# Decoder layer: 18 of 32 gate pairs with seven products, their weight sums made ahead into DRAM scratch

## The chip, the cores and the metric

The kernel runs on one NeuronCore of a Trainium2 chip. The metric is the device time of one execution, in microseconds (us). TensorE is called PE below, VectorE DVE, ScalarE ACT, GpSimd POOL and SyncE SP, as in the profile.

## The reference

One layer of a decoder trunk over T = 16 + 256 positions of width 2048, all in float32:

```python
h = h + 0.5 * swiglu(rms_norm(h, g1), w_gate1, w_up1, w_down1)      # 2048 -> 5632 -> 2048
z = rms_norm(h, g2) @ w_in
q, k, v, qi, ki, wi, xc, gate_b, gate_c, ga, gc = split(z)
y_attn = dsa_sparse_attention(q, k, v, qi, ki, wi, 64) @ w_attn_branch   # indexer, top 64 keys, softmax
y_conv = (gate_b * causal_depthwise_conv(gate_c * xc, conv_w, conv_b)) @ w_conv_branch
h = h + (sigmoid(ga) * y_attn + sigmoid(gc) * y_conv) @ w_out
h = h + 0.5 * swiglu(rms_norm(h, g3), w_gate2, w_up2, w_down2)
return h[:, 16:]
```

The part that matters here is `ga` and `gc`: two projections, 2048 to 2048 each, of the 256 sequence positions, and their merge with the two branch outputs.

## The kernel before, in words

**Weights.** Every weight is streamed from DRAM once, as tiles of 128 partitions x 2048 float32 (1 MiB; 1536 for 768 KB), through three raw buffers, issued on SP's queue (L203). `Stream.split` turns a raw tile, a unit of 128 x 1024 at a time, into a high part `whi` (ACT, L251) and the remainder `wlo` (DVE, L252); a product of weights and activations is then three matmuls (`mac3`, L636 to L638: high by high, high by low, low by high). There are four buffers each for `whi` and `wlo`, and `Stream.next`, called when PE's program comes to a new unit, splits up to three units ahead. What else is to be done is put in lists with a due unit: `early` work is issued before the split of that call, `later` work behind it. All engines run their queues in order.

**Stages.** ffn1 (feature-major, 272 positions wide), the projections for keys, values, indexer and queries with the attention work spread between them, the gated convolution, the gates with the two branch projections, the output projection, ffn2.

**The gates stage.** Four groups c = 0 to 3, each 512 columns of both gates: `pairs_gate(c)` lists eight pairs of row blocks. A pair is a 2 x 2 block product, for two tiles of 128 tokens. A pair of kind `C` is done plainly: 8 block products, 24 matmuls of 512 columns, two units of weights, into the PSUM banks q2, q3, q4, q8. A pair of kind `S` is done with seven products (a Strassen-Winograd scheme): 21 matmuls over three and a half units, 6 matmuls to a full unit, into q1, q5, q6, q7 and q2, q3, q4. It needs sums of the weights, made from the loaded tile by DVE (`sum_ahead`, L223 to L230), and sums of the activations (`made`, made once for each pair index, `sums_of_tokens`). After the last such pair of a group, `recombine` folds the four sum banks into four SBUF tiles: ACT copies q1 (L713), then DVE, one step a unit, reads q6 (L715), q7 (L716), q5 (L717) and q5 again (L718). Behind a group follow 8 units of branch projections (`pbr`, 12 matmuls a unit) into q1, q5 and q6, q7; then `merge` (L1223), issued as early work of the next unit, multiplies these four banks in that order with the sigmoids, and L1225 adds. In groups 1 to 3, between the halves of the seventh pair (n == 6), PE transposes the former group's merged tile into two banks (L683), which ACT and DVE then read out.

**Kind P.** ffn2 has pairs of kind `P` besides: their four weight sums are made ahead, during ffn1, by `Stream.prepare`: a tile is fetched on POOL's queue (L179), DVE adds 4 times 128 x 512 (L183), POOL's queue stores the sums to DRAM scratch (L186). When the pair's turn comes, the 1 MiB of sums and 768 KB of the plain weights are loaded, and there is nothing left to add. Three tiles rotate in `prepare`; a fetch is issued two sets ahead, and the work is spread evenly over the units between two given ones.

The seven products of a pair are issued in this order, where `P` swaps two of them so that q1 is done before q2:

```python
todo7 = [("q7", t3), ("q5", t1), ("q6", t2), ("q3", b22), ("q1", b11), ("q4", t4), ("q2", b21)]
if kind == "P":
    todo7[4:6] = todo7[5:3:-1]
```

Of the kernel before, what the change touches and what calls it, by code (L numbers as in the profile page):

```python
# [24 lines left out]
H = 8  # L25
# [35 lines left out]
SEVEN = (3, 5, 7)  # L61
SEVEN2 = (3, 5, 7, 1)
DOUBLES = 2
SIDE = 6
# [6 lines left out]
def pairs_gate(c):  # L71
    return list(zip("CCCSCSCC", range(PAIRS)) if c == 0 else zip("CSSCSCCC", [0, 3, 5, 1, 7, 2, 4, 6]))
# [24 lines left out]
class Stream:  # L97
# [28 lines left out]
    def add_pair(self, kind, four, five, ahead=None):  # L126

        if kind == "C":
            self.add(four.pop(0), 4, WIDE)
            return  # L130
        if kind == "P":
            src, made = ahead.pop(0)
            self.ahead_of.append(src)
            self.made_ahead.append(made)
            self.add(made, 4, WIDE)
            self.add(src[:, WIDE:], 3, WIDE)
            return
        g = len(self.loads)
        at = 1
        if kind == "D":  # L140
            src, at = five.pop(0), 0
            self.loads.append((src[:, 2 * WIDE :], 3 * WIDE))
            self.added[g] = len(self.doubles)
            self.doubles.append((g, src))
# [62 lines left out]
    def sum_ahead(self):  # L207

        add = self.nc.vector.tensor_add
        for g, kind, _, _, _ in self.subs[self.n_split : self.n_split + 2]:  # L210
            if kind == "sa" and self.sum_pool and g not in self.summed:
# [4 lines left out]
                if g in self.added:  # L216
                    sa, one, last = self.sums[g, "sa"], raw[:, :WIDE], raw[:, 2 * WIDE : 3 * WIDE]
                else:
                    sa, one, last = (
                        self.lent if self.lent is not None else self.sum_pool.tile([P, 2 * WIDE], F32, name="sa", tag="sa"),  # L220
                        raw[:, WIDE : 2 * WIDE], raw[:, 3 * WIDE :],
                    )
                    add(  # L223
                        sa.rearrange("p (q c) -> p q c", q=2),
                        raw[:, WIDE : 3 * WIDE].rearrange("p (q c) -> p q c", q=2),
                        raw[:, :WIDE].rearrange("p (q c) -> p q c", q=1).to_broadcast([P, 2, WIDE]),
                    )
                    self.sums[g, "sa"] = sa
                add(sb[:, :WIDE], sa[:, WIDE:], one)
                add(sb[:, WIDE:], sb[:, :WIDE], last)  # L230
                self.sums[g, "sb"] = sb

    def split(self, upto):
        nc = self.nc
        while self.n_split < min(upto, len(self.subs)):
# [21 lines left out]
            if kind == "sa" and g in self.added:  # L257
# [51 lines left out]
def tile_decoder_layer(  # L309
# [15 lines left out]
    wg: bass.AP,  # L325
    wb: bass.AP,
# [418 lines left out]
    with ExitStack() as mix:  # L745
# [8 lines left out]
        ys = mp.tile([P, H, 2, SEQ], F32R, name="ys")  # L754
        cs = [mp.tile([P, KC // 2, 2, SEQ], F32R, name=f"cs{i}", tag=f"c{i}") for i in range(2)]
# [352 lines left out]

        CV0 = META - 2
# [61 lines left out]
        st.sum_pool = gp  # L1171
# [3 lines left out]
        for at, (i, to) in zip((0, 3, 16), made1.items()):  # L1175
# [16 lines left out]
        def gates(c):  # L1192
# [3 lines left out]
            def after_end(q, buf, tags):  # L1196
# [12 lines left out]
                lambda n: n == 6 and c > 0 and turn_merged(("q6", "q1")), None, after_end,  # L1209
# [22 lines left out]
        st.sum_pool = None  # L1232
# [182 lines left out]
    "h", "small", "rope", "cbias", "ident", "wgu1", "wd1", "wk", "wkw", "wv", "wqi", "wq", "wcv", "wg", "wb",  # L1415
# [30 lines left out]
def _quads(kind, w0, w1, i, j0, j1):  # L1446
# [4 lines left out]
        {"C": [a12, a11, a22, a21], "S": [a21, a11, a22, a12], "P": [a21, a22, a11, a12], "D": [a21, a21, a11, a22, a12]}[kind], 1  # L1451
# [3 lines left out]
def _by_kind(chunks):  # L1455
    return [np.stack([x for k, x in chunks if k in kinds]) for kinds in ("CS", "D", "P")]


def _gates(ga, gc):
    return np.stack([_quads(k, ga, gc, i, c, c) for c in range(D // WIDE) for k, i in pairs_gate(c)])  # L1460


def _second(wg, wu, wd):
# [8 lines left out]
    return _by_kind(res)  # L1472
# [25 lines left out]
def _layout(x, meta_tokens, ffn1_norm_g, ffn1_w_gate, ffn1_w_up, ffn1_w_down, mix_norm_g, w_in, q_norm_g,  # L1498
# [29 lines left out]
    a["wg"] = _gates(ga, gcv)  # L1528
# [26 lines left out]
```

## Time and profile before

| | us |
|---|---|
| median of 3 runs | 2134.0 (2133.54 to 2134.19) |
| the profiled execution | 2133.74 |
| its span | 2131.9 |
| PE busy | 2118.5 |
| DVE busy | 1580.6 |
| ACT busy | 1100.0 |

In the span, ffn1 lies at 0 to 793 us, the key, value, indexer and query projections at 793 to 925, the convolution at 925 to 1087, the gates with the branches at 1087 to 1344, the output projection to 1435, and ffn2 behind it. Rows of the timeline give the start in the span, the duration, the engine, the line and the operation with output and inputs; idle time before it and who ended it stand in brackets. Windows give for each stretch its length, then busy time and count of instructions by engine, granted clock, share of the DMA engines and GB/s. Matmuls are pipelined: the duration of one is longer than the distance from one start to the next.

### The profile page before, as it was taken

The page shows a single profiled execution, that of the slowest core. Times are in us where ns is not written, and L with a number is a line of the kernel's source. Part 1 is how long each engine was busy: PE and PEld are TensorE (multiplying, and loading weights), DVE is VectorE, ACT ScalarE, POOL GpSimd, SP SyncE. Part 2 cuts the span into 40 slices and gives each one's busy share as a digit, 9 for nine tenths or more (in the row PEclk, how much of TensorE's full clock was granted, in tenths as well). Part 3 has the DMA queues.
Part 4 walks back from the last instruction along what each step waited for, and adds up shares of the span by engine and source line. Part 5 has one row for each costly group of instructions (what it writes and reads, how often), then busy time and mean ns, then how long its engine had stood idle before and what let it go on. Part 6 is the DMA issues. An engine that isn't in the chain of part 4 may idle for free.

```text
span 2131.9 us, 32318 instructions
## 1 busy us (share of the span) xinstructions
PE 2118.5 (99%) x13015; PEld 1911.0 (90%) x13015; DVE 1580.6 (74%) x2047; ACT 1100.0 (52%) x1421; POOL 97.6 (5%) x146
## 2 busy tenths in 40 slices
PE   8999999999999999999999999999999999999999
PEld 8999999999999999889988888888888888888887
DVE  7766666666666756577678778587888878888887
ACT  6444433344444445465455555467665566655564
POOL 3000000000000100000000000010000000000000
PEclk9999999999999999999999999999999999999999
DMA  7778888787888854544455565567787887788774
GB/s 283 267 296 308 309 311 298 296 310 306 311 298 296 311 204 165 178 139 159 158 178 188 188 217 195 174 228 251 287 295 243 278 293 275 253 251 304 264 257 148
DMA packets 79927, 531.44 MB, mean 249 GB/s; under 512 B 8896, under 2 KB 9024, under 8 KB 24352
## 3 DMA queue, kind: packets, MB, share of 16 engines
q1 hardware_dynamic: 65088, 432.30, 56.1%
q0 software_dynamic: 14544, 96.89, 13.6%
q8 instruction: 102, 1.67, 0.3%
q14 instruction: 49, 0.40, 0.1%
q10 hardware_dynamic: 144, 0.17, 0.0%
HBM read 483.20 MB, written 46.14 MB: 248 GB/s over the span
## 4 chain that ended last, share of the span: by engine, by line
PE 97%; DVE 1%; ACT 1%; POOL 1%; DMA 0%; issue 0%; SPq 0%; DVEq 0%
PE q L637 13%; PE q L638 13%; PE q L636 13%; PE pd L429 4%; PE pd L430 4%; PE pd L428 4%; PE pg L428 4%; PE pu L428 4%; PE pu L429 4%; PE pg L429 4%; PE pg L430 4%; PE pu L430 4%; PE po L443 3%; PE po L445 1%; PE pbr L636 1%; PE pbr L638 1%
## 5 line engine op out<-in xcount | busy, mean ns | idle before, releaser
L252 DVE TENSOR_TENSOR wlo<-raw,whi 128x1024 fp32r<-128x1024 f32 (+1 forms) x837 | 969.6, 1171 | 504.2 <-ACT whi L251 492.9
L251 ACT ACTIVATE whi<-raw 128x1024 fp32r<-128x1024 f32 (+1 forms) x837 | 842.7, 1015 | 896.7 <-PE q L638 261.1
L636 PE MATMUL q<-whi,act 128*128 128x512 f32 x783 | 305.9, 391 | 0.0
L637 PE MATMUL q<-wlo,act 128*128 128x512 f32 x783 | 305.0, 390 | 0.0
L638 PE MATMUL q<-whi,act 128*128 128x512 f32 x783 | 304.7, 389 | 0.0
L428 PE MATMUL pd<-mid,whi 128*128 128x272 f32 x704 | 201.7, 286 | 0.0
L429 PE MATMUL pd<-mid,whi 128*128 128x272 f32 x704 | 201.7, 286 | 0.0
L430 PE MATMUL pd<-mid,wlo 128*128 128x272 f32 x704 | 201.7, 286 | 0.0
L428 PE MATMUL pg<-act,whi 128*128 128x272 f32 x672 | 192.7, 287 | 0.0
L429 PE MATMUL pg<-act,whi 128*128 128x272 f32 x672 | 192.5, 287 | 0.0
L430 PE MATMUL pg<-act,wlo 128*128 128x272 f32 x672 | 192.5, 286 | 0.0
L428 PE MATMUL pu<-act,whi 128*128 128x272 f32 x672 | 192.5, 286 | 0.0
L429 PE MATMUL pu<-act,whi 128*128 128x272 f32 x672 | 192.5, 286 | 0.0
L430 PE MATMUL pu<-act,wlo 128*128 128x272 f32 x672 | 192.5, 286 | 0.0
L637 PEld LDWEIGHTS q<-wlo,act 128*128 128x128 f32 x783 | 147.1, 188 | 30.8 <-DVE wlo L252 0.9
L638 PEld LDWEIGHTS q<-whi,act 128*128 128x128 f32 x783 | 147.0, 188 | 30.3
L636 PEld LDWEIGHTS q<-whi,act 128*128 128x128 f32 x783 | 147.1, 188 | 30.0
L428 PEld LDWEIGHTS pd<-mid,whi 128*128 128x128 f32 x704 | 132.6, 188 | 0.0
L429 PEld LDWEIGHTS pd<-mid,whi 128*128 128x128 f32 x704 | 132.6, 188 | 0.0
L430 PEld LDWEIGHTS pd<-mid,wlo 128*128 128x128 f32 x704 | 132.6, 188 | 0.0
L429 PEld LDWEIGHTS pg<-act,whi 128*128 128x128 f32 x672 | 126.6, 188 | 0.0
L428 PEld LDWEIGHTS pg<-act,whi 128*128 128x128 f32 x672 | 126.6, 188 | 0.0
(283 smaller groups left out, 3800.4 us busy)
## 6 DMA issues: line engine op xcount, KB each, us to landing
raw<-in_wgu_dram SPq DMA_DIRECT2D x87, 1024.0 KB, 6.1
raw<-in_w_dram SPq DMA_DIRECT2D x74, 1024.0 KB, 6.8
raw<-in_wd_dram SPq DMA_DIRECT2D x44, 1024.0 KB, 6.0
prep<-in_w2p_dram POOLq DMA_DIRECT2D x42, 1024.0 KB, 9.0
sums<-prep POOLq DMA_DIRECT2D x42, 1024.0 KB, 5.5
raw<-sums SPq DMA_DIRECT2D x42, 1024.0 KB, 5.2
raw<-in_wg_dram SPq DMA_DIRECT2D x32, 1024.0 KB, 4.8
raw<-in_w2p_dram SPq DMA_DIRECT2D x42, 768.0 KB, 5.0
```

Of the source, the lines that this page charges most:

```text
L251: nc.scalar.activation(to[0], raw, AF.Copy)
L252: nc.vector.tensor_sub(to[1], raw, to[0].bitcast(F32))
L428: nc.tensor.matmul(ps, whi, xhi, start=first, stop=False)
L429: nc.tensor.matmul(ps, whi, xlo, start=False, stop=False)
L430: nc.tensor.matmul(ps, wlo, xhi, start=False, stop=last)
L443: nc.tensor.matmul(ps.rearrange("p (a t) -> p a t", a=2), whi, x(i), start=i == 0, stop=False)
L445: nc.tensor.matmul(ps[:, :SEQ], wlo, x(i)[:, 0, :], start=False, stop=i == total - 1)
L636: nc.tensor.matmul(ps, xhi, whi, start=n == 0, stop=False)
L637: nc.tensor.matmul(ps, xhi, wlo, start=False, stop=False)
L638: nc.tensor.matmul(ps, xlo, whi, start=False, stop=n == total - 1)
```

## The change

Kind `S` is gone: all pairs with seven products in the gates are now of kind `P`, and there are more of them: three of eight in group 0 (before two), five of eight in each of groups 1 to 3 (before three). The order of the pairs changes with it; groups 1 to 3 now begin with two `P`, and the last one with seven products is the sixth of its group (before the fifth, in group 0 the sixth both times). Sums of activations are made for two more pair indices, 1 and 6, during group 0. `prepare` has 60 sets in place of 42: the 18 of the gates and the first 33 of ffn2's during ffn1, ffn2's last 9 during the key and query projections, in the memory that `cs` and `ys` take afterwards. The transposes of the merged tile go to q1 and then q6, in place of q6 and then q1.

```diff
-SEVEN = (3, 5, 7)
+SEVEN = (3, 5, 7, 1, 6)
+LATE = 9
...
 def pairs_gate(c):
-    return list(zip("CCCSCSCC", range(PAIRS)) if c == 0 else zip("CSSCSCCC", [0, 3, 5, 1, 7, 2, 4, 6]))
+    return list(zip("CCCPPPCC", [0, 2, 4, 3, 5, 7, 6, 1]) if c == 0 else zip("PPCPPPCC", [3, 5, 0, 7, 1, 6, 2, 4]))
...
-    def prepare(self, pool, u0, u1):
+    def prepare(self, tile_of, n0, n1, u0, u1):
...
-        todo = list(zip(self.ahead_of, self.made_ahead))
+        todo = list(zip(self.ahead_of, self.made_ahead))[n0:n1]
...
-                if g in self.added:
-                    sa, one, last = self.sums[g, "sa"], raw[:, :WIDE], raw[:, 2 * WIDE : 3 * WIDE]
-                else:
...
-                add(sb[:, :WIDE], sa[:, WIDE:], one)
-                add(sb[:, WIDE:], sb[:, :WIDE], last)
+                add(sb[:, :WIDE], self.sums[g, "sa"][:, WIDE:], raw[:, :WIDE])
+                add(sb[:, WIDE:], sb[:, :WIDE], raw[:, 2 * WIDE : 3 * WIDE])
...
         for kind, _ in pairs_gate(c):
-            st.add_pair(kind, wg_c, [])
+            st.add_pair(kind, wg_c, [], wg_p)
...
-            st.prepare(fp, 14, units1 - 12)
+            st.prepare(
+                lambda i: fp.tile([P, RAW], F32, name="prep", tag="prep", bufs=3),
+                0, len(st.ahead_of) - LATE, 14, units1 - 12,
+            )
...
+        st.prepare(
+            lambda i: mp.tile([P, RAW], F32, name="prep", tag=("c0", "c1", "ys")[i % 3]),
+            len(st.ahead_of) - LATE, len(st.ahead_of), units1 + 2, units2 - 1,
+        )
...
+        while st.prep:
+            st.prep.pop(0)[1]()
+        ys = mp.tile([P, H, 2, SEQ], F32R, name="ys", tag="ys")
+        cs = [mp.tile([P, KC // 2, 2, SEQ], F32R, name=f"cs{i}", tag=f"c{i}") for i in range(2)]
...
         made1 = {i: gp.tile([P, 2, 4 * P], F32R, name=f"made{i}") for i in SEVEN}
-        for at, (i, to) in zip((0, 3, 16), made1.items()):
+        for at, (i, to) in zip((0, 3, 7, 14, 20), made1.items()):
...
-                lambda n: n == 6 and c > 0 and turn_merged(("q6", "q1")), None, after_end,
+                lambda n: n == 6 and c > 0 and turn_merged(("q1", "q6")), None, after_end,
```

Three places where the order of instructions moves. Line numbers in the changed kernel are lower by 9 in the matmuls and by 16 in the splits; the merge is at L1223 in both.

The first is PE's queue at the start of group 1, from the last branch matmul on. Before (q_12265 is the bank q2, q_12266 is q3):

```order
L638 MATMUL pbr<-whi,cs_8839 128x512
L636 MATMUL q_12265<-whi,act 128x512
L637 MATMUL q_12265<-wlo,act 128x512
L638 MATMUL q_12265<-whi,act 128x512
L636 MATMUL q_12266<-whi,act 128x512
```

And now (q_12428 is q7, q_12446 is q5):

```order
L629 MATMUL pbr<-whi,cs_10177 128x512
L627 MATMUL q_12428<-whi,made_11920 128x512
L628 MATMUL q_12428<-wlo,made_11920 128x512
L629 MATMUL q_12428<-whi,made_11920 128x512
L627 MATMUL q_12446<-whi,made_11920 128x512
```

Before, the first four matmul groups of a gate group went to q2 and q3; now the first goes to q7, the bank in which the branch projection has just ended. On DVE the four multiplications of the merge stand at the same place in both.

The second is DVE's queue from the recombination of group 1 to the end of that group. Before:

```order
L715 TENSOR_TENSOR vv<-q_12328,va 128x512
L252 TENSOR_TENSOR wlo<-raw,whi 128x1024
L716 TENSOR_TENSOR vx<-q_12309,vv 128x512
L252 TENSOR_TENSOR wlo<-raw,whi 128x1024
L717 TENSOR_TENSOR vv<-q_12324,vv 128x512
L252 TENSOR_TENSOR wlo<-raw,whi 128x1024
L718 SCALAR_TENSOR_TENSOR ve<-q_12324,vx 128x512
L465 TENSOR_TENSOR ms_12536<-pt,ms_12536 128x4x128 x2
```

And now:

```order
L706 TENSOR_TENSOR vv<-q_12450,va 128x512
L236 TENSOR_TENSOR wlo<-raw,whi 128x1024
L707 TENSOR_TENSOR vx<-q_12428,vv 128x512
L453 TENSOR_TENSOR ms_12707<-pt,ms_12707 128x4x128 x2
L236 TENSOR_TENSOR wlo<-raw,whi 128x1024
L708 TENSOR_TENSOR vv<-q_12446,vv 128x512
L1198 TENSOR_TENSOR va<-q_12476,va 128x512
```

The reading of the transposes (`ms`) now comes two units earlier against the recombination: PE's transposes into q1 and q6 stand one unit behind the end of the last seven products, where they stood three units behind it.

The third is DVE's queue in the last unit ahead of the branches of group 0. Before:

```order
L717 TENSOR_TENSOR vv<-q_11915,vv 128x512
L1198 TENSOR_TENSOR va<-q_11782,va 128x512
L1198 TENSOR_TENSOR vv<-q_11783,vv 128x512
L252 TENSOR_TENSOR wlo<-raw,whi 128x1024
L718 SCALAR_TENSOR_TENSOR ve<-q_11915,vx 128x512
```

And now:

```order
L708 TENSOR_TENSOR vv<-q_12065,vv 128x512
L1198 TENSOR_TENSOR va<-q_11935,va 128x512
L1198 TENSOR_TENSOR vv<-q_11936,vv 128x512
L236 TENSOR_TENSOR wlo<-raw,whi 128x1024
L652 TENSOR_TENSOR vm_11934<-vm_11933 128x256
L653 TENSOR_TENSOR vm_11934<-vm_11933,vm_11934 128x128
L654 TENSOR_TENSOR vm_11934<-vm_11933,vm_11934 128x128
L709 SCALAR_TENSOR_TENSOR ve<-q_12065,vx 128x512
```

Three additions for the activation sums of pair index 6 now stand ahead of the last reading of q5.

More of the change, by code (lines that the diff above doesn't have):

```diff
@@ L138, in add_pair @@
         g = len(self.loads)
[L139 to L144, printed above, removed]
-        else:
-            self.loads.append((four.pop(0), RAW))
+        src = five.pop(0)
+        self.loads.append((src[:, 2 * WIDE :], 3 * WIDE))
+        self.added[g] = len(self.doubles)
+        self.doubles.append((g, src))
         self.subs += [
             (g, "sa", 0, 2, WIDE), (g, "sb", 0, 2, WIDE),
-            (g, "one", at * WIDE, 2, WIDE), (g, "last", (at + 2) * WIDE, 1, WIDE),
+            (g, "one", 0, 2, WIDE), (g, "last", 2 * WIDE, 1, WIDE),
         ]
@@ L177, in fetch @@
             if i < len(todo):
-                tiles[i] = pool.tile([P, RAW], F32, name="prep", tag="prep", bufs=3)
+                tiles[i] = tile_of(i)
                 nc.gpsimd.dma_start(tiles[i], todo[i][0])
@@ L256, in split @@
             self.n_split += 1
-            if kind == "sa" and g in self.added:
+            if kind == "sa":
                 self.add_up(self.added[g] + 1 + DOUBLES)
@@ L363, in tile_decoder_layer @@
     chunks(wq, 0, 8, 512)
+    units2 = len(st.subs)
     chunks(wcv, 0, 3 * KC)
-    wg_c, w2_c, w2_d, w2_p = ([w[i] for i in range(w.shape[0])] for w in (wg, w2, w2d, w2p))
+    wg_c, wg_p, w2_c, w2_d, w2_p = ([w[i] for i in range(w.shape[0])] for w in (wg, wgp, w2, w2d, w2p))
     scratch = ctx.enter_context(tc.tile_pool(name="scratch", bufs=1, space=bass.MemoryType.DRAM))
-    w2_p = [(w, scratch.tile([P, RAW], F32, name=f"sums{i}")) for i, w in enumerate(w2_p)]
+    wg_p, w2_p = (
+        [(w, scratch.tile([P, RAW], F32, name=f"{s}{i}")) for i, w in enumerate(ws)] for s, ws in (("sg", wg_p), ("s2", w2_p))
+    )
     for c in range(D // WIDE):
         for kind, _ in pairs_gate(c):
-            st.add_pair(kind, wg_c, [])
+            st.add_pair(kind, wg_c, [], wg_p)
         for i in range(KC // 2):
@@ L753, in tile_decoder_layer @@
         qT = mp.tile([P, H, SEQ], F32, name="qT", tag="tB")
-        ys = mp.tile([P, H, 2, SEQ], F32R, name="ys")
-        cs = [mp.tile([P, KC // 2, 2, SEQ], F32R, name=f"cs{i}", tag=f"c{i}") for i in range(2)]
+        mp.tile([P, H, 2, SEQ], F32R, name="ys", tag="ys")
+        for i in range(2):
+            mp.tile([P, KC // 2, 2, SEQ], F32R, name=f"cs{i}", tag=f"c{i}")
+        st.prepare(
+            lambda i: mp.tile([P, RAW], F32, name="prep", tag=("c0", "c1", "ys")[i % 3]),
+            len(st.ahead_of) - LATE, len(st.ahead_of), units1 + 2, units2 - 1,
+        )
         short = mix.enter_context(ExitStack())
@@ L1414 @@
 _INS = [
[L1415 removed]
+    "h", "small", "rope", "cbias", "ident", "wgu1", "wd1", "wk", "wkw", "wv", "wqi", "wq", "wcv", "wg", "wgp", "wb",
     "wo", "w2", "w2d", "w2p",
@@ L1450, in _quads, with _by_kind @@
     return np.concatenate(
[L1451 removed]
+        {"C": [a12, a11, a22, a21], "P": [a21, a22, a11, a12], "D": [a21, a21, a11, a22, a12]}[kind], 1
     )
[L1455 to L1456 removed]
+def _by_kind(chunks, kinds):
+    return [np.stack([x for k, x in chunks if k == kind]) for kind in kinds]
 def _gates(ga, gc):
[L1460 removed]
+    return _by_kind([(k, _quads(k, ga, gc, i, c, c)) for c in range(D // WIDE) for k, i in pairs_gate(c)], "CP")
 def _second(wg, wu, wd):
```

20 lines of the change are left out of this document (4 added, 16 removed).

## The prediction

> **What bounds the kernel now.** The page first: busy time by engine and the chain that ended last.
>
> ```profile
> PE 2118.5 (99%) x13015; PEld 1911.0 (90%) x13015; DVE 1580.6 (74%) x2047; ACT 1100.0 (52%) x1421; POOL 97.6 (5%) x146
> ...
> PE 97%; DVE 1%; ACT 1%; POOL 1%; DMA 0%; issue 0%; SPq 0%; DVEq 0%
> ```
>
> PE is the bound from end to end, so a matmul that is left out is worth its time, and each time PE waits for a bank or a weight is lost in full. Next the windows by stage (ffn1, projections, their densest stretch, gates).
>
> ```profile
> 40.00:793.00 753.00, 753.00 (x6108) 753.00 (x6107) 504.52 (x656) 311.42 (x375) 50.03 (x89) 1.00 0.78 292
> 793.00:925.00 132.00, 132.00 (x747) 112.10 (x746) 84.34 (x174) 66.86 (x104) 2.14 (x4) 1.00 0.51 175
> 890.00:920.00 30.00, 30.00 (x150) 23.11 (x149) 24.55 (x53) 14.86 (x19) 0.00 (x0) 1.00 0.43 149
> 1087.00:1344.00 257.00, 256.57 (x1143) 211.74 (x1142) 201.07 (x224) 140.05 (x158) 0.48 (x1) 1.00 0.57 194
> ```
>
> PE is idle 0.43 us in the whole gates stage and never in the first two. So there is no stall in the gates that a lighter DVE could remove: the DVE additions that go with kind S were hidden already, and only PE's work can be gained. What a matmul costs is read from the timeline, between two that are 24 apart:
>
> ```profile
> 1194.16 0.39 PE L636 MATMUL pbr<-whi,ys 128*128 128x512 f32 x1
> ...
> 1199.60 0.39 PE L636 MATMUL pbr<-whi,ys 128*128 128x512 f32 x1
> ```
>
> 5.44 us over 24 is 0.2267 us from start to start. The 0.39 us is the latency of one; counted with it, the gain would come out too large by 1.7 times.
>
> **The change part by part.**
>
> *PE's work.* Seven pairs more have 21 matmuls in place of 24 (3 + 3 x 5 = 18 against 2 + 3 x 3 = 11): 21 matmuls fewer, 21 x 0.2267 = **-4.8 us**. [...]
>
> *The start of groups 1 to 3* (the first order piece). The first matmul now writes q7, and q7 still holds the branch product that the merge reads as the last of its four. The same place in the trace of before, PE's rows and then DVE's:
>
> ```profile
> 1151.48 0.39 PE L638 MATMUL pbr<-whi,cs 128*128 128x512 f32 x1
> 1151.71 0.39 PE L636 MATMUL q<-whi,act 128*128 128x512 f32 x1
> ...
> 1150.33 1.23 DVE L252 TENSOR_TENSOR wlo<-sa,whi 128x1024 fp32r<-128x1024 f32 x1 [0.54 <-ACT whi L251]
> 1151.48 0.68 DVE L1223 TENSOR_TENSOR va<-pbr,va 128x512 f32<-128x512 f32 x1
> 1152.08 0.68 DVE L1223 TENSOR_TENSOR vv<-pbr,vv 128x512 f32<-128x512 f32 x1
> 1152.67 0.68 DVE L1223 TENSOR_TENSOR vx<-pbr,vx 128x512 f32<-128x512 f32 x1
> 1153.27 0.68 DVE L1223 TENSOR_TENSOR ve<-pbr,ve 128x512 f32<-128x512 f32 x1
> ```
>
> q7's reader ends at 1153.95, while PE went on at 1151.71 with q2. The four readers stand behind a wlo that had itself waited 0.54 us for its whi; that order is unchanged, so they do not come earlier. The other two places:
>
> ```profile
> 1215.92 0.39 PE L636 MATMUL q<-whi,act 128*128 128x512 f32 x1
> ...
> 1217.49 0.68 DVE L1223 TENSOR_TENSOR ve<-pbr,ve 128x512 f32<-128x512 f32 x1
> ...
> 1280.16 0.39 PE L636 MATMUL q<-whi,act 128*128 128x512 f32 x1
> ...
> 1281.72 0.68 DVE L1223 TENSOR_TENSOR ve<-pbr,ve 128x512 f32<-128x512 f32 x1
> ```
>
> 18.17 against 15.92 and 82.40 against 80.16: 2.25 us each time. What PE adds behind a DVE release is shown by the one stall of this stage, at the branches of group 0:
>
> ```profile
> 1127.42 0.68 DVE L1198 TENSOR_TENSOR va<-q,va 128x512 f32<-128x512 f32 x1
> ...
> 1128.62 1.22 DVE L252 TENSOR_TENSOR wlo<-raw,whi 128x1024 fp32r<-128x1024 f32 x1
> 1129.75 0.68 DVE L718 SCALAR_TENSOR_TENSOR ve<-q,vx 128x512 f32<-128x512 f32 x1
> ...
> 1129.67 0.39 PE L638 MATMUL pbr<-whi,ys 128*128 128x512 f32 x1
> 1130.49 0.50 PE L636 MATMUL pbr<-whi,ys 128*128 128x512 f32 x1 [0.43 <-DVE ve L718]
> ```
>
> 0.05 us from ve's end to the matmul, which then takes 0.50 in place of 0.39. So 2.25 + 0.05 + 0.1 = 2.4 us, three times: **+7.2 us**. Without the 0.1 it is 6.9; that it is nothing at all is a rival below.
>
> *The transposes of groups 1 to 3* (the second piece). They now come one unit behind the last seven products. In the trace of before that last block ends at 1176.93, where the plain unit starts:
>
> ```profile
> 1176.93 0.39 PE L636 MATMUL q<-whi,act 128*128 128x512 f32 x1
> ...
> 1179.65 0.39 PE L636 MATMUL q<-whi,act 128*128 128x512 f32 x1
> ...
> 1185.10 1.03 PE L683 MATMUL pt<-ident,vm 128*128 128x128 f32 x8
> ...
> 1176.45 1.06 ACT L251 ACTIVATE whi<-raw 128x1024 fp32r<-128x1024 f32 x1 [0.30 <-PE q L638]
> 1177.41 0.58 ACT L713 ACTIVATE va<-q 128x512 f32<-128x512 f32 x1
> ...
> 1178.97 1.23 DVE L252 TENSOR_TENSOR wlo<-raw,whi 128x1024 fp32r<-128x1024 f32 x1 [0.20 <-ACT whi L251]
> 1180.11 0.69 DVE L715 TENSOR_TENSOR vv<-q,va 128x512 f32<-128x512 f32 x1
> ```
>
> Moved there, PE would want q1 at 1179.65, long after its copy (1177.99), and q6 some 0.45 later, at 1180.10; q6's reader ends at 1180.80. Wait 0.75, with the restart 0.85 us: that is the lower end. It grows if the whi and wlo ahead of that reader are late, which the loads decide (next part). The raw buffer for the plain tile after next comes free when the first load of the third P is split: PE must be through with the unit four before, 30 matmuls or 6.8 us ahead of 1176.93, then come about 0.2 us, a whi (1.06) and a wlo (1.23), so 4.2 us ahead. With 4.8 us to land it is there at +0.6; two whi, a wlo and the reader (0.69) then end at +4.6, where PE wants q6 at +3.2: 1.6 us with the restart. I take 1.4, nearer the upper end since the loads are dense there: 3 x 1.4 = **+4.2 us**, from 2.6 to 4.8.
>
> *Loads of three P in a row.*
>
> ```profile
> raw<-sums SPq DMA_DIRECT2D x42, 1024.0 KB, 5.2
> raw<-in_wg_dram SPq DMA_DIRECT2D x32, 1024.0 KB, 4.8
> ```
>
> A P needs two loads in 21 x 0.2267 = 4.76 us of PE, where S needed one. A raw buffer is taken for about 4.8 us of landing and 3.4 (one whi, two wlo, from the rows above) or, for the smaller load, 2.9 us of splitting: 15.9 us a pair over three buffers, 5.3 us. So each P runs 0.5 us short; three are 1.6 us short, against some 1 to 2 us of units and tiles in hand. In each of four groups 0 to 0.8 us; I take 0.3: **+1.2 us**, from 0 to 3.2. The splits themselves (about 4 us of DVE to 4.76) fit.
>
> *Group 0's branches* (the third piece). The stall quoted above, about 0.7 us, grows by the three additions now ahead of ve, less the 0.69 us of a made tile that no longer delays the unit. In the rows of before they are
>
> ```profile
> 1123.50 0.42 DVE L661 TENSOR_TENSOR vm<-vm 128x256 f32<-128x256 f32 x1
> ...
> 1124.28 0.29 DVE L663 TENSOR_TENSOR vm<-vm,vm 128x128 f32<-128x128 f32 x1
> ```
>
> 1.0 us together: +0.3 to +1.0, taken **+0.7 us**.
>
> *Sets made ahead.* Nine more in ffn1 move 9 x 2 MiB = 18.9 MB in 753 us, 25 GB/s on 292 (share 0.78 to about 0.85), and 36 additions of
>
> ```profile
> L183 DVE TENSOR_TENSOR prep<-prep 128x512 f32<-128x512 f32 x168 | 115.0, 684 | 0.0
> ```
>
> 25 us on 505 of 753. PE has no idle time there and three units of weights in hand, so **0**. The nine between 793 and 925 put as much on DVE's 84 of 132 us, and on the 24.6 of 30 us around 905 about nine additions, 6 us: DVE is full there. It may fall some 2 us behind; weights three units ahead (over 8 us) hide that: **0**, or up to 4 us if an indexer step on PE has to wait for DVE. POOL's queue has the fetches and stores ahead of one memset that ACT waits for; DVE makes the sums one unit earlier. The gates' DVE loses 11 sums and gains splits; PE waits for neither.
>
> Sum: -4.8 + 7.2 + 4.2 + 1.2 + 0.7 = **+8.5 us**, on the profiled 2133.74 us; that execution is 0.3 us under the median, so I put it on the median, 2134.0: **2142.5 us**. The forecast's own range, its ends added up: -4.8 + 6.9 + 2.6 + 0 + 0.3 = +5 to -4.8 + 7.2 + 4.8 + 3.2 + 1.0 = +11.4, 2139 to 2145.4.
>
> **The rivals.** A change under 0.2% (4.3 us) can hardly be told from none here: same is 2129.7 to 2138.3.
>
> *The merge comes early.* DVE without S's sums gets to the merge while PE is still in the branches. Place: the first L1223 of groups 0 to 2. It decides if that starts before about 1150.2 in the trace's time, when q1's last product is done. The four reads would follow the four banks, and q7 would be free one read (0.68) and a latency (0.39) after the last matmul started at 1151.48: 1152.6, a wait of 0.9. With the other terms at their low ends, -4.8 + 3 x 1.0 + 2.6 + 0.3 = +1: 2135, no slower. For it: 11 sums gone. Against: the wlo ahead of the merge had waited for whi, not for sums. 15%.
>
> *No wait at all*: the bank is not in PE's way, nor are the transposes: -4.8, 2129 us. Against: the order rows put q7 first. 6%.
>
> *DVE full in the query projection*: the 4 us above on top, 2146.5. For: 24.6 of 30 before any addition. Against: PE's idle of 0 and its three units. 8%.
>
> *The clock falls.* At the program's start PE runs at half pace until about 13 us:
>
> ```profile
> 12.46 0.43 PE L430 MATMUL start<-act,wlo 128*128 128x272 f32 x1
> 12.69 0.43 PE L428 MATMUL start<-act,whi 128*128 128x272 f32 x1
> ...
> 13.67 0.29 PE L428 MATMUL start<-act,whi 128*128 128x272 f32 x1
> 13.79 0.29 PE L429 MATMUL start<-act,whi 128*128 128x272 f32 x1
> ```
>
> 0.23 us a matmul, then 0.12: over the 6 us from the first matmul it loses about 2.8 us. Were the 2.2 us of idle enough to bring that back, three times: +8.4, 2151. 5%. [...]
>
> **How the numbers follow.** Forecast 63%, the early merge 15%, no wait 6%, DVE full 8%, the clock 5%, and 3% for a delay elsewhere, as a fetch in ffn1 that lands late (+5 and more). Faster: 0.06. Same: the early merge and a little of the rest, 0.17. Slower: 0.77. The range reaches down to the early merge and up nearly to the clock: 2135 to 2150.
>
> **What would show it.** PE idle of 2.1 to 2.3 us at the first q matmul behind pbr in groups 1 to 3, released by DVE ve L1223; 0.4 to 1.5 us at the transposes behind DVE L706; the stall behind DVE ve L709 in group 0 longer than 0.43; PE rows 21 fewer; ffn1 and the projections without PE idle. It is wrong if the first of these is missing, or if PE idles between 793 and 925.

## The result, and the profile after

| | median, us | lowest to highest | ratio to before, 95% interval |
|---|---|---|---|
| before, beside the change | 2133.8 | 2133.5 to 2134.2 | |
| the change | 2162.2 | 2159.2 to 2167.4 | 1.0135 (1.0114 to 1.0156) |

The change is 28.4 us slower, where +8.5 was forecast, and it lies above the range (2135 to 2150). Its executions also differ by 8 us among themselves, those of before by 0.7. The profiled execution, the slowest of the four, took 2167.35 us, its span 2165.6 (before 2131.9): 33.7 us have to be accounted for in that execution. Where one execution of a set below was disturbed and took at least a fifth longer, medians and ranges leave it out.

The page of the changed kernel, busy time by engine and the chain that ended last:

```profile
PE 2129.0 (98%) x12994; PEld 1913.1 (88%) x12994; DVE 1611.4 (74%) x2108; ACT 1112.2 (51%) x1441; POOL 117.0 (5%) x182
...
PE 89%; DVE 4%; DMA 4%; ACT 2%; issue 1%; POOL 0%; SPq 0%; ACTq 0%; DVEq 0%; POOLq 0%
```

PE has 21 instructions fewer, as computed, and yet 10.5 us more busy time: some of its matmuls ran slower. The chain, which was PE for 97%, now passes through DVE, ACT and DMA for a tenth. The same stages in windows (the columns are PE, PEld, DVE, ACT, POOL busy with counts, then the granted clock, the DMA share and GB/s):

```profile
40.00:793.00 753.00, 753.00 (x6108) 753.00 (x6107) 525.58 (x692) 311.07 (x375) 59.62 (x106) 1.00 0.84 317
793.00:930.50 137.50, 134.35 (x749) 114.02 (x748) 104.70 (x208) 66.91 (x105) 11.84 (x22) 0.99 0.81 297
1092.60:1378.40 285.80, 265.66 (x1124) 212.96 (x1123) 191.04 (x214) 152.65 (x178) 0.59 (x1) 0.97 0.64 224
```

ffn1 is as full as before. From the first matmul of one stage to that of the next, the gates take 285.8 us in place of 257.5 (+28.3), and the query projection 58.5 in place of 53.5 (+5.0); the rest agrees within 0.6 us. So two stages hold the whole loss, and in both the granted clock is under 1.00. What PE waited for (line, who released it; us in total, times, longest):

```profile
PE q L627 <- DVE ve L1223: 6.5, 3, 2.2
PE pt L674 <- DVE vv L706: 6.2, 3, 2.1
PE q L628 <- DVE wlo L236: 3.8, 5, 0.8
PE pqt L904 <- DVE zz L807: 3.4, 2, 3.2
PE pbr L627 <- DVE ve L709: 1.9, 1, 1.9
PE q L627 <- ACT whi L235: 1.5, 4, 0.6
```

From the top: PE at the start of groups 1 to 3 behind the merge, the transposes of groups 1 to 3, weights that come late, the query's transposes (3.15 us of it in one gap at 883.5), and group 0's branches. The second to the fifth were forecast too small, and one thing comes on top that these lines do not show. This is the timeline of PE behind one of the merge's gaps:

```profile
1305.85 0.47 PE L627 MATMUL q<-whi,made 128*128 128x512 f32 x1 [2.18 <-DVE ve L1223]
1306.15 0.40 PE L628 MATMUL q<-wlo,made 128*128 128x512 f32 x1
1306.39 0.39 PE L629 MATMUL q<-whi,made 128*128 128x512 f32 x1
1306.62 0.56 PE L627 MATMUL q<-whi,made 128*128 128x512 f32 x1
1306.97 0.63 PE L628 MATMUL q<-wlo,made 128*128 128x512 f32 x1
1307.40 0.63 PE L629 MATMUL q<-whi,made 128*128 128x512 f32 x1
...
1309.54 0.63 PE L628 MATMUL q<-wlo,act 128*128 128x512 f32 x1
1309.96 0.46 PE L629 MATMUL q<-whi,act 128*128 128x512 f32 x1
1310.26 0.39 PE L627 MATMUL q<-whi,made 128*128 128x512 f32 x1
```

PE starts again at full pace (0.23 us from start to start), and 0.8 us later goes over to 0.43 us for about 3.4 us, with nothing to wait for. By the rows a stretch holds about 8 matmuls where 15 would have stood, and costs 1.6 to 1.7 us. The granted clock tells the same: it is 0.50 in all of this window, and 1.00 before and behind it.

```profile
1306.69:1310.09 3.40, 3.40 (x10) 2.63 (x9) 1.75 (x3) 1.06 (x1) 0.00 (x0) 0.50 0.46 128
```

There are six such stretches in this execution, five in the gates and one at 883.5, about 10 us in all. The account of the gates, from start to start of the rows (each matmul's distance to the next, above 0.2267 us), by the row that released the wait: merge 7.3, transposes 6.9, late weights 7.9, group 0's branches 2.2 (before 0.7), half pace 8.3 in five stretches, less 4.8 for the matmuls: 27.1 of the 28.3.

### The profile page after: what moved, and what is told of

The parts are those of the page before. It is cut to its first block, busy times and chain, and to the rows that moved or that the text cites. A ratio compares the mean times of both kernels' runs of the same rounds, so it can differ in the third digit from the quotient of the medians.

```text
span 2165.6 us, 32506 instructions
## 1 busy us (share of the span) xinstructions
PE 2129.0 (98%) x12994; PEld 1913.1 (88%) x12994; DVE 1611.4 (74%) x2108; ACT 1112.2 (51%) x1441; POOL 117.0 (5%) x182
## 4 chain that ended last, share of the span: by engine, by line
PE 89%; DVE 4%; DMA 4%; ACT 2%; issue 1%; POOL 0%; SPq 0%; ACTq 0%; DVEq 0%; POOLq 0%
PE q L627 12%; PE q L629 12%; PE q L628 12%; PE pd L418 4%; PE pd L416 4%; PE pd L417 4%; PE pu L417 4%; PE pu L418 4%; PE pu L416 4%; PE pg L417 4%; PE pg L418 4%; PE pg L416 4%; PE po L431 3%; DVE wlo L236 2%; PE po L433 1%
## 5 line engine op out<-in xcount | busy, mean ns | idle before, releaser
L236 DVE TENSOR_TENSOR wlo<-raw,whi 128x1024 fp32r<-128x1024 f32 (+1 forms) x873 | 1007.6, 1168 | 502.9 <-ACT whi L235 493.0
L235 ACT ACTIVATE whi<-raw 128x1024 fp32r<-128x1024 f32 (+1 forms) x873 | 875.0, 1013 | 927.4 <-PE q L629 248.0
L628 PE MATMUL q<-wlo,act 128*128 128x512 f32 x748 | 293.1, 392 | 2.4 <-DVE wlo L236 2.3
L627 PE MATMUL q<-whi,act 128*128 128x512 f32 x748 | 294.2, 393 | 0.8 <-ACT whi L235 0.8
L629 PE MATMUL q<-whi,act 128*128 128x512 f32 x748 | 292.7, 391 | 0.0
L628 PEld LDWEIGHTS q<-wlo,act 128*128 128x128 f32 x748 | 141.5, 189 | 32.6 <-DVE wlo L236 3.8
L627 PEld LDWEIGHTS q<-whi,act 128*128 128x128 f32 x748 | 141.6, 189 | 30.9 <-ACT whi L235 1.9
L180 DVE TENSOR_TENSOR prep<-prep 128x512 f32<-128x512 f32 x240 | 164.2, 684 | 5.5 <-DMA prep<-in_w2p_dram 5.5
L629 PEld LDWEIGHTS q<-whi,act 128*128 128x128 f32 x748 | 141.3, 189 | 29.7
L416 PEld LDWEIGHTS pg<-act,whi 128*128 128x128 f32 x672 | 126.6, 188 | 0.0
```

Source lines behind the costliest of these rows:

```text
L180: nc.vector.tensor_add(x[out], x[a], x[b])
L235: nc.scalar.activation(to[0], raw, AF.Copy)
L236: nc.vector.tensor_sub(to[1], raw, to[0].bitcast(F32))
L416: nc.tensor.matmul(ps, whi, xhi, start=first, stop=False)
L627: nc.tensor.matmul(ps, xhi, whi, start=n == 0, stop=False)
L628: nc.tensor.matmul(ps, xhi, wlo, start=False, stop=False)
```

## The experiments

The kernel before stood at 2133.5 to 2133.7 us beside the runs (medians of each set). The first six kernels are edits of the changed kernel; what the others start from is said there.

**Are the sums from scratch themselves the cost?** The control has before's eleven pairs and orders, with the weight sums loaded from DRAM scratch in place of those that DVE makes at the pair's turn. Within a pair the order is that of kind P, q4 ahead of q1; q1 comes ahead of q2 in both kinds.

```diff
-SEVEN = (3, 5, 7, 1, 6)
+SEVEN = (3, 5, 7)
...
-LATE = 9
+LATE = 0
...
-    return list(zip("CCCPPPCC", [0, 2, 4, 3, 5, 7, 6, 1]) if c == 0 else zip("PPCPPPCC", [3, 5, 0, 7, 1, 6, 2, 4]))
+    return list(zip("CCCPCPCC", range(PAIRS)) if c == 0 else zip("CPPCPCCC", [0, 3, 5, 1, 7, 2, 4, 6]))
...
-        for at, (i, to) in zip((0, 3, 7, 14, 20), made1.items()):
+        for at, (i, to) in zip((0, 3, 16), made1.items()):
...
-                lambda n: n == 6 and c > 0 and turn_merged(("q1", "q6")), None, after_end,
+                lambda n: n == 6 and c > 0 and turn_merged(("q6", "q1")), None, after_end,
```

> The eleven seven-product pairs of before at before's places, with the transposes and the order of q4 and q1 of before, but their sums come from DRAM scratch (kind P in place of S), made in ffn1. Theory 'the sums from scratch cost nothing, only the new places do': PE's work and waits as before, 2133 to 2135. Rival 'the second load of a pair is itself the cost': eleven loads of 1 MiB more, each up to 0.8 us short on three buffers: 2138 to 2143.

Measured: 2133.50 us (2132.72 to 2134.27), ratio 1.0000 (0.9990 to 1.0009). PE's waits from the gates on are one, the same as before:

```profile
PE pbr L627 <- DVE ve L709: 0.4, 1, 0.4
```

So at before's places kind P costs and gains nothing that could be told from the noise. What is left for the loss is what else the change does: the number and the places of the pairs, and the sets made late.

**The late sets.**

```diff
-LATE = 9
+LATE = 0
```

> All 60 sets of sums are made in ffn1, none during the key and query projections. Theory 'a fetch that lands late blocks the queue of DVE': the 3.15 us of idle at the query's transposes go, with the half clock behind it and the later start of the next stage 5.1 us: 2156 to 2158, and the convolution's stage starts about 5 us earlier against the start of the query projection. Rival 'DVE and the transfers are full in ffn1 as well': nine sets more in a narrower room push PE idle into ffn1, and the time stays at 2162 or rises to 2168.

Measured: 2154.75 us (2150.99 to 2157.69), ratio 1.0099 (1.0084 to 1.0114), 7.4 us less than the change and 1.2 us below the theory's range. PE has no wait between 793 and 930 us, and ffn1 takes all 60 sets without PE idle. The query projection takes 53.55 us (change 58.5, before 53.54), so it gives back the 5 us that the theory said; the rest of the 7.4 is within the spread of the executions. How the late set stopped PE is read in the changed kernel's timeline, first POOL's queue, then DVE, then PE:

```profile
863.38 0.53 POOL L176 DMA_DIRECT2D prep<-in_w2p_dram  x1
...
872.91 1.23 DVE L236 TENSOR_TENSOR wlo<-raw,whi 128x1024 fp32r<-128x1024 f32 x1 [2.81 <-ACT whi L235]
879.61 0.69 DVE L180 TENSOR_TENSOR prep<-prep 128x512 f32<-128x512 f32 x1 [5.48 <-DMA prep<-in_w2p_dram]
...
883.09 0.28 DVE L807 TENSOR_TENSOR zz<-rot 128x128 f32<-128x128 f32 x1
...
883.52 3.55 PE L904 MATMUL pqt<-ident,zz 128*128 128x128 f32 x16 [3.15 <-DVE zz L807]
```

The view of that fetch says who waited for it, and how long it took:

```profile
  DVE prep L180: 5.5, 1
...
DMA to landing us min/median/max: 16.2/16.2/16.2
```

It goes out at 863.4, two sets ahead and without waiting for anything, and lands at 879.6; the median of the stage's fetches is 10.1 us. The addition that needs it is next in DVE's queue, and all of DVE stands for 5.48 us, a wlo and the rotation of the query behind it. PE runs dry at 880.4 and starts at 883.5. What stood beside that fetch is seen in the windows of that stretch, before and then with the change:

```profile
855.00:880.00 25.00, 25.00 (x115) 20.44 (x115) 13.63 (x21) 11.03 (x17) 0.00 (x0) 1.00 0.54 192
855.00:880.00 25.00, 25.00 (x113) 20.22 (x111) 16.07 (x31) 11.03 (x17) 2.14 (x4) 1.00 0.97 381
```

The DMA engines go from 0.54 busy to 0.97. The stores issued at 862.85 and 870.40 took 12 us too (median 7.8), and the query's weights up to 12.0, where 4.9 is their median before. So fetches, stores and weights all took longer where they stood together; whether the late weights alone would have stopped PE here is not separated.

**Is it the transfer, or DVE's work?** The forecast's rival was a full DVE. Here DVE does the 36 additions of the nine late sets in the same stretch, on three tiles of zeros (`blank` makes them, `add_blank` adds), and nothing is fetched or stored.

```diff
-LATE = 9
+LATE = 0
...
-        st.prepare(
-            lambda i: mp.tile([P, RAW], F32, name="prep", tag=("c0", "c1", "ys")[i % 3]),
-            len(st.ahead_of) - LATE, len(st.ahead_of), units1 + 2, units2 - 1,
-        )
...
+        st.prep = [(u0, blank)] + [(u0 + 4 + n * (u1 - u0 - 4) // 36, lambda n=n: add_blank(n)) for n in range(36)]
```

> All sets of sums are made in ffn1, as in the kernel with LATE = 0, but DVE does the 36 additions of the key and query projections all the same, at the same places, on three tiles of zeros; no fetch and no store goes with them, and nobody reads the result (the layer's output does not depend on it). Theory 'a fetch that lands late blocks DVE's queue': DVE's work alone costs nothing, PE has no idle in the query projection, and the time is that of LATE = 0, 2151 to 2158, with the convolution's first matmul at about 924.9 us. Rival 'DVE is full there': PE waits for zz at the query's transposes for 2 us and more, the convolution starts at 929 to 931 us, and the time is that of the change, 2158 to 2163.

Measured: 2155.06 us (2151.22 to 2159.85), ratio 1.0109 (1.0092 to 1.0126). PE has no wait in the projections, and the convolution starts at 924.73 us. The whole stage, and its densest 30 us:

```profile
793.00:924.80 131.80, 131.80 (x745) 111.97 (x744) 104.38 (x209) 66.84 (x103) 7.32 (x7) 1.00 0.51 173
890.00:920.00 30.00, 30.00 (x150) 23.09 (x149) 28.56 (x61) 14.85 (x19) 0.00 (x0) 1.00 0.44 148
```

DVE is busy for 28.56 of 30 us and PE loses nothing. The rival falls: DVE's load was harmless, the transfers were not.

**The banks.**

```diff
-            sides = [[[bank(tag, "pbr"), 0, KC] for tag in tags] for tags in (("q1", "q5"), ("q6", "q7"))]
+            sides = [[[bank(tag, "pbr"), 0, KC] for tag in tags] for tags in ((("q6", "q3"), ("q1", "q2")) if c < 3 else (("q1", "q5"), ("q6", "q7")))]
```

> Only the banks of the branch sums of groups 0 to 2 are others (q6, q3 and q1, q2 in place of q1, q5 and q6, q7). It takes away PE's idle 3 x 2.18 us behind ve of the merge and 1.92 us behind ve of group 0, 8.5 us, and about 0.2 us of restart each. Theory 'the waits add up': about 9.3 us less, and 1.6 us less for each of up to three stretches at half clock that stood behind these gaps: 2148 to 2153, with the other PE waits as they are. Rival 'the three raw buffers bound the three P in a row': the gaps had given the loads time; without them PE waits at the wlo and whi of the second and third P, 0.5 to 1.3 us more in each group, and 5 to 6 us of the gain are given back: 2154 to 2158.

Measured: 2156.75 us (2154.42 to 2157.86), ratio 1.0108 (1.0093 to 1.0123). The waits in its gates:

```profile
PE q L628 <- DVE wlo L236: 7.7, 11, 0.8
PE pt L674 <- DVE vv L706: 5.1, 3, 2.0
PE q L627 <- ACT whi L235: 1.2, 5, 0.3
PE pbr L627 <- DVE ve L709: 0.6, 1, 0.6
```

The 6.5 us behind the merge are gone, and the wait at group 0's branches too (the 0.6 is group 3's); but late weights went from 5.3 us (3.8 and 1.5) to 8.9. The gain is 5.4 us where the two waits had 9.5 by the account above. Time and waits are the rival's: the gaps had been time for the loads. (The mean granted clock of the profiled execution is 0.998 here and 0.995 in the change, so the two also differ in half pace.)

**The transposes.**

```diff
-                lambda n: n == 6 and c > 0 and turn_merged(("q1", "q6")), None, after_end,
+                lambda n: n == 7 and c > 0 and turn_merged(("q1", "q6")), None, after_end,
```

> Only the transposes of groups 1 to 3 are moved one pair later (behind the plain half of pair 7 in place of 6). Theory 'the waits add up': PE's idle of 1.95, 2.15 and 2.15 us behind vv (L706) goes, with restarts about 7 us, and 1.6 us for each stretch at half clock behind them (two in the profile shown): 2151 to 2155. Rival 'the late weights keep DVE behind for longer than a pair': part of the wait is found again at the later place, and the gain is under 4 us: 2157 to 2160.

Measured: 2157.49 us (2153.14 to 2159.91), ratio 1.0107 (1.0090 to 1.0124): 4.7 us less. The time is in the rival's range, the gain a little over the 4 us that the rival allowed. Half of the wait moved on:

```profile
PE pbr L627 <- DVE ms L453: 3.3, 3, 1.4
```

Now the branches want q1 and q6 before DVE has split what was transposed into them. With other banks that should go, which the next kernel has.

**All places mended at once, 18 pairs, three raw buffers.**

```diff
-LATE = 9
+LATE = 0
...
-                lambda n: n == 6 and c > 0 and turn_merged(("q1", "q6")), None, after_end,
+                lambda n: n == 7 and c > 0 and turn_merged(("q7", "q1")), None, after_end,
...
-            sides = [[[bank(tag, "pbr"), 0, KC] for tag in tags] for tags in (("q1", "q5"), ("q6", "q7"))]
+            sides = [[[bank(tag, "pbr"), 0, KC] for tag in tags] for tags in ((("q3", "q6"), ("q2", "q1")) if c < 3 else (("q6", "q5"), ("q1", "q7")))]
```

> The change with its places mended at once: all sets of sums in ffn1; branch sums in q3, q6 and q2, q1 (groups 0 to 2), so that the bank read last by the merge is not the one that the next group writes first; transposes one pair later, in q7 and q1, which the branches want last. 18 pairs as before. Theory 'three raw buffers bound three P in a row': the gaps behind the merge, ve and vv are gone, but PE waits at wlo and whi of the second and third P for some 8 us in all, in steps under 0.8 us; no stretch at half clock: 2136 to 2140. Rival 'it was the banks and the clock alone': PE's idle in the gates is under 2 us and the 21 matmuls fewer are seen: 2129 to 2131.

Measured: 2142.01 us (2141.35 to 2145.78), ratio 1.0043 (1.0028 to 1.0059): 2 us above the theory's range and far from the rival's, with no half-pace stretch in the profile. In the gates PE waits for weights ten times (6.4 us), once for ms, and ACT waits for the loads:

```profile
ACT whi L235 <- DMA raw<-in_wg_dram: 19.6, 10, 3.2
PE q L628 <- DVE wlo L236: 6.2, 9, 0.8
ACT whi L235 <- DMA raw<-sg: 6.0, 5, 2.0
ACT whi L235 <- DMA raw<-in_wb_dram: 3.5, 3, 2.1
ACT whi L235 <- DMA raw<-in_wgp_dram: 3.0, 3, 1.9
PE pbr L627 <- DVE ms L453: 1.5, 1, 1.5
```

The waits of PE sum to 7.9 us (with one of 0.2 not shown), yet the gates take 266.3 us: 8.9 over before and, with 4.8 us less work, 13.6 us of loss. By the rows from start to start the same waits cost 11.6 us (around one of 0.76 us the two distances are 1.26 and 0.34 us, in place of 0.23 each), and 1.9 us are matmuls that start late by less than the 0.39 us that the row of the one ahead lasts, which the profile shows as no wait at all.

**A fourth raw buffer** in that kernel for groups 0 to 2, in the place of a tensor that is dead by then; the merged tile of group 1, transposed, goes where group 2's went, and group 2's into the lent place.

```diff
+        class Lent:
+            def tile(self, shape, dtype, name):
+                return mp.tile(shape, dtype, name=name, tag="tB")
+
+        st.raw_pools, st.raw_bufs, st.n_raw = [Lent()] + [raw_pool] * 3, RAW_BUFS + 1, 0
-        places = [[("tA", 4)], [("tB", 4)], [("zz0", 2), ("zz1", 2)], [("c0", 4)]]
+        places = [[("tA", 4)], [("zz0", 2), ("zz1", 2)], [("tB", 4)], [("c0", 4)]]
...
         for c in range(D // WIDE):
+            if c == 3:
+                st.raw_pools, st.raw_bufs, st.n_raw = [raw_pool], RAW_BUFS, 0
             gates(c)
```

> The kernel with mended places, and a fourth raw buffer in groups 0 to 2 (the place of qT lent to it, the transposed sums of group 1 and 2 put elsewhere for that). Theory 'three raw buffers bound three P in a row': the waits at wlo and whi of groups 0 to 2 go and stay in group 3 alone (2 to 3 us of them): 2130 to 2133. Rival 'the splitting on DVE and ACT bounds, not the loads': the waits stay and the time is that of three buffers, 2136 to 2140.

Measured: 2131.63 us (2130.39 to 2132.78), ratio 0.9991 (0.9982 to 0.9999): 10.4 us less than with three. The same view of its gates:

```profile
ACT whi L235 <- DMA raw<-in_wg_dram: 3.8, 4, 1.4
ACT whi L235 <- DMA raw<-in_wb_dram: 3.1, 3, 1.8
ACT whi L235 <- DMA raw<-in_wgp_dram: 2.0, 1, 2.0
ACT whi L235 <- DMA raw<-sg: 0.6, 1, 0.6
PE q L628 <- DVE wlo L236: 0.5, 1, 0.5
```

32.1 us of ACT waiting for loads became 9.5, of which 6.6 stand in group 3, while the splitting is the same work. The waits of 2 to 3 us that the theory left in group 3 show as 0.5 alone; but from start to start groups 1 and 2, with four buffers, take 63.2 and 63.6 us, and group 3, with three, 65.6. So the raw buffers bound the runs of P, not DVE or ACT.

**Fewer pairs, three buffers.** The kernel with all places mended, with 15 pairs, never more than two P in a row.

```diff
-SEVEN = (3, 5, 7, 1, 6)
+SEVEN = (3, 5, 7, 1)
...
-    return list(zip("CCCPPPCC", [0, 2, 4, 3, 5, 7, 6, 1]) if c == 0 else zip("PPCPPPCC", [3, 5, 0, 7, 1, 6, 2, 4]))
+    return list(zip("CCPPCPCC", [0, 2, 3, 5, 4, 7, 6, 1]) if c == 0 else zip("PCPPCPCC", [3, 0, 5, 7, 2, 1, 4, 6]))
...
-        for at, (i, to) in zip((0, 3, 7, 14, 20), made1.items()):
+        for at, (i, to) in zip((0, 3, 8, 15), made1.items()):
```

> The kernel with mended places and three raw buffers, but with 15 pairs of seven products in place of 18, no more than two in a row (PCPPCPCC, in group 0 CCPPCPCC). PE's work is 12 matmuls under before, 2.7 us. Theory 'three in a row is what three raw buffers cannot feed': the plain pairs between give the loads their time, PE's idle in the gates is under 1.5 us: 2130.5 to 2132.5. Rival 'each P runs 0.5 us short wherever it stands': 15 P lose as much each as 18 do: 2135 to 2138.

Measured: 2133.83 us (2131.64 to 2137.24), ratio 1.0001 (0.9992 to 1.0010). The median lies between the two ranges and meets neither. The profiled execution, 2131.64, is the fastest and has no wait for weights in the gates (one of 0.75 us for ms), as the theory says; the others are up to 5.6 us longer and were not profiled, so what takes the gain back there stays open.

**Behind which gaps does the half pace come?** Three kernels made from the four-buffer one put q7 back among the branch sums of groups 0 to 2, read as the third of the merge's four, as the fourth, and as the fourth behind one addition more. Shown is the part of the line that changes.

```diff
-("q3", "q6"), ("q2", "q1")
+("q3", "q6"), ("q7", "q2")
```

> The four-buffer kernel (2131.6), with the bank q7 put back into the branch sums of groups 0 to 2, there read as the third of the merge's four. PE then waits for it at the start of groups 1 to 3, about 1.55 us each. Theory 'fixed windows': PE goes to half pace for one window of 3.41 us if it was idle for more than about 1.8 us of the window before; a gap of 1.55 cannot fill that, so no stretch at half clock in any execution: 3 x (1.55 + 0.25) = 5.4, 2136 to 2138, runs within 3 us of each other. Rival 'any wait of some length can pull the clock, by chance': stretches of 0.63 us matmuls behind one or two of the three, 2138 to 2141.

```diff
-("q3", "q6"), ("q2", "q1")
+("q3", "q6"), ("q2", "q7")
```

> The same with q7 read as the fourth, as in the change itself: three gaps of 2.15 to 2.2 us. Theory 'fixed windows': a gap of 2.18 us has more than 1.8 us in one window of 3.41 in about 55% of positions, so 0 to 3 stretches at half clock of 1.7 us each, another number in each execution: 3 x 2.4 = 7.2 for the waits, and 2139 to 2144, median 2141 to 2142; each stretch begins on the grid of 3.413 us, and the window before it holds the gap. [...]

```diff
-("q3", "q6"), ("q2", "q1")
+("q3", "q6"), ("q2", "q7")
...
+                nc.vector.tensor_add(m[0], box["q2"], box["q3"])
```

> The same with q7 read as the fourth, and one addition of 0.6 us more on DVE ahead of the merge's four reads (its result is overwritten): three gaps of 2.8 us. Theory 'fixed windows': more than 1.8 us falls into one window in about three of four positions: 3 x 3.05 = 9.2 for the waits and mostly two or three stretches of 1.7 us: 2142 to 2147, median 2144 to 2146. [...]

| q7 read as | gaps, us | time, us (median, range) | ratio to before | half-pace stretches in the gates of the profiled execution |
|---|---|---|---|---|
| third | 1.58, 1.58, 1.58 | 2136.28 (2134.52 to 2137.21) | 1.0011 (1.0002 to 1.0020) | 0 |
| fourth | 2.18, 2.18, 2.18 | 2139.40 (2136.60 to 2142.53) | 1.0027 (1.0018 to 1.0037) | 1 |
| fourth, one addition more | 2.97, 2.97, 2.97 | 2142.68 (2141.23 to 2143.05) | 1.0040 (1.0026 to 1.0055) | 1 |

In the profiled executions none of the gaps of 1.58 us is followed by half pace, one of the three of 2.18 and one of the three of 2.97 are. So 2.18 us of idle was enough once, and two gaps of 2.97 us were followed by none: the length of the gap alone does not decide here. In the second kernel the first of the three equal gaps is the one followed by half pace; its rows, and the granted clock in a window of them:

```profile
1152.48 0.47 PE L627 MATMUL q<-whi,made 128*128 128x512 f32 x1 [2.18 <-DVE ve L1229]
...
1154.08 0.63 PE L627 MATMUL q<-whi,made 128*128 128x512 f32 x1
1154.51 0.63 PE L628 MATMUL q<-wlo,made 128*128 128x512 f32 x1
```

```profile
1154.00:1157.00 3.00, 3.00 (x8) 2.30 (x7) 1.37 (x2) 1.18 (x2) 0.00 (x0) 0.50 0.55 172
```

Where the gaps lie can be read in the changed kernel. Its granted clock is 0.50 in six stretches of 3.41 us. The table gives their beginnings, and PE's idle (length less busy time) in the window of 3.41 us ahead of each:

| half pace from, us | 883.43 | 1139.43 | 1200.87 | 1235.01 | 1306.68 | 1347.64 |
|---|---|---|---|---|---|---|
| PE idle in the 3.41 us ahead, us | 3.06 | 1.92 | 1.95 | 2.18 | 2.18 | 1.98 |

In this execution the beginnings are 75, 18, 10, 21 and 12 times 3.4133 us apart, within 0.02 us. With the span from 20 us on laid out in the same steps, no other step has more than 1.77 us of PE idle. Two of the eight gaps over 1.9 us are not followed by half pace, and in both cases a border of these steps cuts the gap: the one of 2.18 us that ends at 1164.19 falls into two steps with 1.32 and 0.86 us of idle, the one of 2.15 us that ends at 1272.92 into two with 1.77 and 0.38. So in this execution 1.92 us and more within one step was followed by half pace, and 1.77 us was not. For the other kernels the steps are not laid out here, so which of their gaps such a border cuts is not shown.

Two sizes were off. The waits themselves cost 1.55 us each in the first kernel ((2136.28 - 2131.63) / 3) and about 1.9 in the second (its profiled 2138.91 less one stretch of 1.6) where 1.8 and 2.4 were expected, probably because the loads gain by them; and the longest gap brought one stretch in the profiled execution, not two or three, and 2142.7 us, near the lower edge of the range. The profiled execution is the fastest of its four (2141.23, mean granted clock 0.999); the others, not profiled, have 0.998.

**The best of these.** The four-buffer kernel with two edits more:

```diff
+    if c == 3:
+        return list(zip("PCPPCPCC", [3, 0, 5, 7, 2, 1, 4, 6]))
...
-                lambda n: n == 7 and c > 0 and turn_merged(("q7", "q1")), None, after_end,
+                lambda n: n == 7 and c > 0 and turn_merged(("q1", "q7")), None, after_end,
```

> The four-buffer kernel with two small edits: the transposes go to q1 first and then q7, so that q1, which the branches want sooner, is free 0.6 us earlier; and group 3, which has three buffers, gets four pairs of seven, no more than two in a row (PCPPCPCC), 17 pairs in all. Theory 'three buffers cannot feed three P in a row': some 1.8 us of late starts in group 3 go for 0.7 us of PE's work, and 0.5 us at the branches: 2129.5 to 2131.2. Rival 'these waits only move': 2131.4 to 2132.5.

Measured: 2130.39 us (2129.48 to 2131.60), ratio 0.9985 (0.9975 to 0.9994), in the theory's range. It is faster than the kernel before by 3.2 us, of the 4.1 us that its 18 matmuls fewer are worth. In the gates PE has one wait:

```profile
PE q L630 <- DVE wlo L238: 0.7, 1, 0.7
```

## Why the prediction was wrong

**Direction and first mechanism right.** PE is idle 2.18 us at the first q matmul of groups 1 to 3, released by ve of the merge; 2.1 to 2.3 was written. With restarts it is 7.3 us against +7.2. The 21 matmuls are gone as computed, and ffn1 shows no PE idle. Matmuls of 512 columns are 0.227 us apart at full pace with the change too (24 of them from 1143.48 to 1148.93 us). But the prediction's own sign of being wrong, PE idle between 793 and 925 us, is there, 3.15 us of it. In the profiled execution the terms came out as: matmuls -4.8 (forecast -4.8), merge 7.3 (7.2), transposes 6.9 (4.2), loads 7.9 (1.2), group 0's branches 1.5 (0.7), half pace in the gates 8.3 (0), late sets 5.0 (0); together 32.1 of the 33.7 us.

**The step that failed most: what a stall costs.** Each was priced as idle time plus 0.1 us of restart. The clock stood as a rival at 5%, for the three merge gaps alone, at 2.8 us each. That their 2.2 us would be too short was my estimate, and no run showed it: the longest PE gap in the gates of before is 0.43 us. Behind six of the eight gaps over 1.9 us the clock fell, 1.6 to 1.7 us each: about 10 of the 33.7 us of that execution. It is the slowest of the four, with a mean granted clock of 0.995; the others have 0.996 to 0.998, so by my estimate the median holds fewer stretches. I had weighed a gap by its length alone, and not asked where it lies: in the changed kernel 1.92 us within one of the steps above was enough, and a gap of 2.18 us cut in two was not.

**Loads of three P in a row, +1.2 (0 to 3.2).** The balance of 15.9 us over three buffers was the right mechanism, but it was mis-sized. One piece is seen: the plain tiles (`in_wg_dram`) landed in 6.1 us (median, gates), where 4.8 went into the balance; how much of the reserve "in hand" was there is not shown. In the change late weights cost 7.9 us from start to start, and that while the other gaps gave the loads time; with the other places mended, a fourth buffer is worth 10.4 us.

**Transposes, +4.2 (2.6 to 4.8).** Measured 6.9, over the upper end, plus two half-pace stretches. The bound was built on a raw buffer that lands 0.6 us late; with weights later than that, the reader of q6 (vv, L706) came later on DVE. In groups 1 and 2 the whi two ahead of it had waited 1.2 and 1.4 us for its load (`in_wg_dram`), in group 3 1.5 us for a wlo. So the mis-sized loads entered a second time here.

**Group 0's branches, +0.7.** The wait went from 0.43 to 1.92 us, +1.5 in place of +0.7 by the rows from start to start. DVE's rows there:

```profile
1136.17 1.22 DVE L236 TENSOR_TENSOR wlo<-raw,whi 128x1024 fp32r<-128x1024 f32 x1
1137.30 0.42 DVE L652 TENSOR_TENSOR vm<-vm 128x256 f32<-128x256 f32 x1
...
1138.29 0.68 DVE L709 SCALAR_TENSOR_TENSOR ve<-q,vx 128x512 f32<-128x512 f32 x1
```

The three additions take the 1.0 us that was counted. The 0.69 us of a made tile that I set against them were not given back, and the wlo ahead stands some 0.5 us later against PE than before.

**"Sets made ahead: 0", in the projections.** The cost was 5.0 us in that stage. I had asked whether DVE has the capacity (it has) and whether weights three units ahead cover a lag of 2 us. I did not price the transfers there, which take the DMA engines from 0.51 to 0.81 busy over the stage and to 0.97 between 855 and 880 us, nor follow a fetch that lands late to the addition that stands in order on DVE in front of a wlo and the rotation. The rival "DVE full in the query projection" named the stage and nearly the price, but not the cause.

## What to carry to other kernels

In the changed kernel one addition that waited for its transfer held up all that stood behind it on DVE, for 5.48 us. So work made ahead must be priced by when its data lands, not by the engine's busy share (DVE busy for 28.56 of 30 us cost PE nothing), and the DMA engines' share, here 0.97, belongs to the price. With PE as the bound, a gap could cost more than its length: behind six of the eight over 1.9 us in the change stood half pace, 1.6 to 1.7 us more each, while three of 1.58 us cost nothing beyond themselves. And the stalls did not add up: with other banks 5.4 us came back of the 9.5 that the two waits had, since the next limit (here the three raw buffers) showed. Each single edit left 21 us or more of the loss, the places mended together 8, and only with the fourth raw buffer did the kernel become faster.

## What was not expected of the hardware

PE went to half pace in the middle of the program, behind gaps of about 2 us. In the changed kernel's profiled execution it did so six times, for 3.41 us each, with the granted clock at 0.50 and beginnings that are multiples of 3.4133 us apart; the 3.41 us ahead of each held 1.92 to 3.06 us of PE idle. Where the pace changes at the start of the program differs between profiled executions: by the rows matmuls go from 0.23 to 0.12 or 0.13 us apart at 13.0 us in the change and at 12.3 us with blank additions. The changed kernel's executions lie 8 us apart, those of before 0.7. That the number of stretches makes the spread was not counted execution by execution, since one of each kernel was profiled; but the mean granted clock of the executions falls with their time, from 1.000 at 2136.6 us to 0.998 at 2142.5 in the kernel with 2.18 us gaps, and from 1.000 at 2151.2 to 0.997 at 2159.9 in the one with blank additions.
